# Phase one with kept weights, a later sigmoid, a copied z and B and C in a tile of their own

## The chip, the core and the metric

The kernel runs on one core of a Trainium2 chip. Its engines are TensorE (PE; the loading of its weights is PEld), VectorE (DVE), ScalarE (ACT), GpSimd (POOL) and SyncE (SP), which here issues all transfers in one queue. Each engine works through its own list of instructions in order. The metric is the device time of one execution in microseconds.

## The reference, cut to what matters

One layer of a streaming encoder on 2048 prompt frames and 32 frames of a running stream. The change lies in the first half, where the normalised input is multiplied by one input projection and the results go to two groups of heads.

```python
proj = rmsnorm(x, g_mix_pre) @ w_in            # 1024 -> q, k, v, z, xBC, dt
xbc_c = silu(causal_dwconv(xbc, ...))          # 768 channels: x 512, B 128, C 128; four taps
y = ssd_scan(x, dt, a, B, C, h0) + d_skip * x  # chunks, state carried on
y = rmsnorm(y * silu(z), g_ssm_out)
attn = stick_breaking(q, k_all, v_all)
out = concat(rmsnorm(attn, g_attn_out), y) @ w_out   # then residual, conv FFN
```

## The kernel before, in words

All products are made in pairs of halves: every operand is cut into a high part and the rest (hi, lo), and a product takes three matmuls (hi hi, lo hi, hi lo). The tokens lie along the free dimension, in four superblocks of 512, 512, 512 and 544 columns.

**Phase one** (`phase_in`, L253) runs over the superblocks. For each it

1. splits the normalised input into xhi and xlo (`split`, L315; superblock 0 in `first`, which multiplies by the norm r0 only behind the matmuls, because the norm is not there yet),
2. makes the six units of 128 channels of x, B and C, in the order 4 (B), 5 (C), 0 to 3 (x): 24 matmuls into a PSUM tile `o` of two buffers, an exit by ScalarE to `raw` (L377), a four-tap convolution on VectorE into `xc` (one `tensor_scalar`, L384, and three `scalar_tensor_tensor`, L388), a sigmoid on ScalarE (L392) and a product on VectorE (L393),
3. makes v and dt for four blocks of 128 tokens ("V", L412), two accumulators of 24 matmuls per block, each left by ScalarE (L419 or L421), in the same two buffers `o`,
4. runs the state-space scan over the blocks (`y`, `st`, `acB`, `eA`), woven into
5. the matmuls of k and q (eight units), while `prep` (L294) loads and normalises the next superblock's input,
6. makes the four units of z (`gate`, L609): a sigmoid on ScalarE and a product on VectorE both read z in PSUM (L627, L628), and a second product puts it on `xc` (L630),
7. normalises `xc` (`gate_norm`, L635) and stores it to `yS`. Only then is `xc` free for the next superblock's convolution, for it has one buffer.

The last superblock's z and norm run later, in phase two, which holds attention and the FFN.

**Weights.** `weight` (L106) fetches a unit: `raw` loads 512 KB into `wraw` (two buffers, L122), and `divide` makes the high half on ScalarE (a cast, L145) and the low half on GpSimd (a subtraction, L146), into `w` (two buffers in phase one). If a key is given, `divide` also writes both halves (1 MB) to a scratch tensor in DRAM, and a later `weight` with the same key loads them back with `recall` (L132), without ScalarE and GpSimd. In phase one no unit had a key.

**Order.** A scheduler sets the order of the instructions on each engine from the program, its dependencies and a model of durations; the order on the chip is then fixed.

Of the kernel before, what the change touches and what calls it, by code (L numbers as in the profile page):

```python
# [45 lines left out]
NSB = len(SBS)  # L46
# [23 lines left out]
class Kernel:  # L70
# [182 lines left out]
def phase_in(kn, ctx):  # L253
    nc, tc, a, o = kn.nc, kn.tc, kn.a, kn.o
# [5 lines left out]
    tmp = pool("in_tmp", 2)  # L260
    so = pool("in_out", 2)
    wp = kn.wp
# [90 lines left out]

    wfirst = kn.weight(wp, a["wbx"][4])
    for s, (t0, nt) in enumerate(SBS):
        last = s == NSB - 1
        if s == 0:
            xs, r0 = first()
            rcol = kn.rcol
# [3 lines left out]
        raw = ep.tile([P, 6, 550], F32, name="raw")  # L363
        xc = kn.xcp.tile([P, 6, 547], F32, name="xc")
        W = 547 if last else 512
        nc.vector.tensor_copy(raw[:, :, 0:3], hist[:])
        if last:
            nc.vector.tensor_copy(
                raw[:, :, 515:518], kn.cv[:, C_SST : C_SST + 18].rearrange("p (c t) -> p c t", t=3)
            )  # L370
        for c in (4, 5, 0, 1, 2, 3):
            w = wfirst if s == 0 and c == 4 else kn.weight(wp, a["wbx"][c])
            for c0, c1 in tiles_of(nt):
                ps = psd.tile([P, 512], F32, name="o")
                kn.dense(ps, w, xs, c0, c1)
                e = min(c1, 512)
                nc.scalar.copy(raw[:, c, 3 + c0 : 3 + e], ps[:, : e - c0])  # L377
                if c1 > 512:
                    nc.scalar.copy(raw[:, c, 518:550], ps[:, e - c0 : c1 - c0])
            if s == 0:  # L380
                nc.vector.tensor_tensor(raw[:, c, 3 : 3 + nt], raw[:, c, 3 : 3 + nt], r0[:, :nt], op=ALU.mult)
            y = xc[:, c, :W]
            wc = C_SW + c * 4
            nc.vector.tensor_scalar(  # L384
                y, raw[:, c, 0:W], kn.col(wc), kn.col(C_SB + c), op0=ALU.mult, op1=ALU.add
            )
            for i in range(1, 4):
                nc.vector.scalar_tensor_tensor(  # L388
                    y, raw[:, c, i : i + W], kn.col(wc + i), y, op0=ALU.mult, op1=ALU.add
                )  # L390
            t = tmp.tile([P, 550], F32, name="t")
            nc.scalar.activation(t[:, :W], y, AF.Sigmoid)  # L392
            nc.vector.tensor_tensor(y, y, t[:, :W], op=ALU.mult)  # L393
        if last:
# [11 lines left out]
        for b in range(nb):  # L406
            q = min(P, nt - b * P)
            vp = [psd.tile([P, 512], F32, name="o") for _ in range(2)]
            for h in range(2):
                for k in range(KC):  # L410
                    for i, (l, rr) in enumerate(((xhi, wv[0]), (xlo, wv[0]), (xhi, wv[1]))):
                        nc.tensor.matmul(  # L412
                            vp[h][:q, :260], l[k][:, b * P : b * P + q], rr[:, k, h * 260 : h * 260 + 260],
                            start=i == 0 and k == 0, stop=i == 2 and k == KC - 1,
                        )
            v = sd.tile([P, 520], F32, name="v")
            for dst, src in ((v[:q, 0:260], vp[0][:q, :260]), (v[:q, 260:520], vp[1][:q, :260])):
                if s == 0:
                    nc.scalar.activation(dst, src, AF.Copy, scale=rcol[:q, b : b + 1])  # L419
                else:  # L420
                    nc.scalar.copy(dst, src)  # L421
            nc.vector.tensor_tensor(
# [32 lines left out]
        ps = psm.tile([P, 512], F32, name="st")  # L455
# [17 lines left out]
        for b in range(nb):  # L473
            q = min(P, nt - b * P)
# [21 lines left out]
            for g in range(2):  # L496
                rows = slice(g * 64, g * 64 + 64)
                nc.tensor.matmul(cy[:q, g, :q], xc[rows, 4, sl], xc[rows, 5, sl], start=True, stop=True)
                for i in range(2):
                    nc.tensor.matmul(  # L500
                        cy[:, g, P + i * q : P + i * q + q],
                        h_in[rows, 2 * i : 2 * i + 2, :].rearrange("p h d -> p (h d)"), xc[rows, 5, sl],
                        start=True, stop=True,
                    )
# [26 lines left out]
            ps = psm.tile([P, 512], F32, name="st")  # L531
            nc.tensor.transpose(ps[:q, :P], xc[:, 4, sl], kn.ident[:])
            bT = sd.tile([P, P], F32, name="bT")
# [62 lines left out]
        if last:  # L596
# [3 lines left out]
            )  # L600
        bufs = {"khi": 2, "klo": 2, "t": 2, "sq": 1}
        tm = lambda nm: (so if nm in ("khi", "klo") else tmp).tile([P, 550 if nm == "t" else 544], F32, name=nm, bufs=bufs[nm])
# [6 lines left out]
def gate(kn, s, xs, xc, r0, tm):  # L609
# [3 lines left out]
    for c in range(4):  # L613
        w = kn.weight(kn.wp, kn.a["wz"][c])
        for c0, c1 in tiles:
# [7 lines left out]
            if r0 is not None:  # L623
                z = tm("t")
                nc.vector.tensor_tensor(z[:, :n], ps[:, :n], r0[:, c0:c1], op=ALU.mult)
                ps = z
            nc.scalar.activation(t[:, :n], ps[:, :n], AF.Sigmoid)  # L627
# [844 lines left out]
def build(nc, tc, a, o):  # L1472
    kn = Kernel(nc, tc, a, o)
    with ExitStack() as ctx:
# [17 lines left out]
        with ExitStack() as c2:  # L1492
            kn.wp, kn.unit, kn.wbufs, kn.rbufs = c2.enter_context(tc.tile_pool(name="weights_in", bufs=1)), KC, 2, 2
            rest = phase_in(kn, c2)
# [125 lines left out]
```

## Time and profile before

| what | us |
|---|---|
| median of three runs (lowest, highest) | 2935.15 (2931.43, 2939.62) |
| the profiled execution | 2941.02 |
| its span | 2939.2 |
| TensorE busy in the span | 2814.1 |

A row of busy time by stage has the stage, its length, then for each engine busy time and count of instructions, the granted TensorE clock, the DMA share and GB/s. A row of waits has the waiting engine, tile and line, what it waited for, and total, times and longest in us. A row of a timeline has start, duration, engine, line, operation, tiles, count, and in brackets the idle time ahead of it and what ended it. A group has busy time, mean ns of one, then idle time ahead of it and its causes. A row of the chain of waits has start, duration and what ran. Names like L161 are lines of the kernel before.

### The profile page before, as it was taken

Reading aid. Unit: us, or ns where it says so; the run is one execution under the profiler, and the core shown is the slowest. Engines: PE = TensorE matmul, PEld = TensorE weight load, DVE = VectorE, ACT = ScalarE, POOL = GpSimd, SP = SyncE. Lnnn points to the kernel's source line nnn. Section 1 sums busy time; section 2 is a strip of 40 time slices with the busy share of each in tenths; the row PEclk is TensorE's granted clock in tenths of the full one; section 3 lists DMA queues with packets and bytes.
Section 4 is the critical chain, followed back from the end, with each engine's and each line's share of the span. In section 5 each row is a group of like instructions: output and inputs, shape, how many; then the busy total and the mean of one; then the engine's idle time right before and its main releaser. Section 6 shows DMA issues by size and latency. Waiting matters only on the chain.

```text
span 2939.2 us, 46252 instructions
## 1 busy us (share of the span) xinstructions
PE 2814.1 (96%) x16771; PEld 2427.5 (83%) x16771; DVE 1690.8 (58%) x2628; ACT 1263.4 (43%) x2622; POOL 1275.4 (43%) x1131
## 2 busy tenths in 40 slices
PE   7999999989889999999999999999999999999997
PEld 6777777977788888897788888977888889999997
DVE  7667586566773555447555556675666653623333
ACT  4344444337665555446333444654444443321111
POOL 4565555435766666656322323453223233511113
PEclk9999999989999999999999999999999999999999
DMA  5646464648787778777655556656555445765556
GB/s 179 183 137 193 132 176 124 174 115 271 247 282 263 253 263 276 266 256 250 215 180 172 174 180 219 225 182 205 176 172 170 160 159 202 241 181 179 170 178 200
DMA packets 333093, 586.47 MB, mean 200 GB/s; under 512 B 73306, under 2 KB 192738, under 8 KB 332866
## 3 DMA queue, kind: packets, MB, share of 16 engines
q1 hardware_dynamic: 332866, 583.52, 62.1%
q8 instruction: 134, 2.20, 0.3%
q14 instruction: 93, 0.76, 0.1%
HBM read 445.70 MB, written 137.69 MB: 198 GB/s over the span
## 4 chain that ended last, share of the span: by engine, by line
PE 72%; DVE 13%; DMA 7%; ACT 3%; issue 2%; POOL 1%; SPq 1%; DVEq 0%; ACTq 0%; POOLq 0%
PE o L161 35%; PE u L161 12%; PE t L161 10%; PE z L863 4%; PE pa L904 4%; PE pt L882 3%; DVE xc L388 2%; DMA acB<-acD 2%; PE o L412 1%; DVE acB L488 1%; DVE prow L714 1%; DMA xr<-hS 1%; DVE xc L384 1%; DVE xlo L320 1%; DVE x L310 1%
## 5 line engine op out<-in xcount | busy, mean ns | idle before, releaser
L161 PE MATMUL o<-xhi,w 128*128 128x512 f32 (+2 forms) x3968 | 1047.9, 346 | 24.1 <-ACT xhi L334 8.0
L161 PEld LDWEIGHTS o<-xhi,w 128*128 128x128 f32 x3968 | 697.3, 191 | 119.0 <-ACT xhi L334 8.0
L161 PE MATMUL o<-xlo,w 128*128 128x512 f32 (+2 forms) x1984 | 683.8, 345 | 6.3 <-DVE xlo L320 4.2
L146 POOL TENSOR_TENSOR w<-wraw,w 128x512 fp32r<-128x512 f32 (+3 forms) x244 | 384.3, 1577 | 261.4 <-ACT w L145 232.2
L719 POOL TENSOR_TENSOR beta<-beta,prow 128x512 f32<-128x512 f32 (+3 forms) x256 | 252.5, 987 | 442.7 <-DVE prow L714 366.8
L161 PEld LDWEIGHTS o<-xlo,w 128*128 128x128 f32 x1984 | 380.0, 192 | 50.4 <-DVE xlo L320 6.1
L161 PE MATMUL u<-xhi,w 128*128 128x512 f32 x1056 | 350.3, 398 | 0.0
L161 PE MATMUL o<-ah,w 128*128 128x512 f32 x992 | 344.4, 403 | 4.3 <-DVE f L1348 3.8
L1300 POOL TENSOR_TENSOR y<-y,gb 128x512 f32<-128x512 f32 (+1 forms) x88 | 116.0, 1318 | 503.2 <-ACT gb L1299 503.1
L714 DVE TENSOR_TENSOR_SCAN prow<-gam,prow,z 128x513 f32<-128x513 f32 x192 | 245.2, 1278 | 74.1 <-ACT beta L712 69.7
L887 DVE TENSOR_TENSOR wt<-pt,wt 128x512 fp32r<-128x512 f32 (+2 forms) x320 | 191.0, 602 | 159.6 <-ACT wt L886 157.8
L886 ACT CAST wt<-pt 128x512 fp32r<-128x512 f32 (+2 forms) x320 | 166.9, 527 | 218.2 <-PE pt L882 216.3
L145 ACT CAST w<-wraw 128x512 fp32r<-128x512 f32 (+3 forms) x244 | 172.1, 705 | 170.6 <-PE o L161 98.6
L161 PEld LDWEIGHTS u<-xhi,w 128*128 128x128 f32 x1056 | 199.1, 189 | 46.8
L161 PEld LDWEIGHTS o<-ah,w 128*128 128x128 f32 x992 | 187.2, 189 | 47.0 <-DVE f L1348 6.0
L711 ACT ACTIVATE gam<-z 128x512 f32<-128x512 f32 (+2 forms) x320 | 172.3, 538 | 96.0 <-PE z L863 53.9
L161 PE MATMUL u<-xlo,w 128*128 128x512 f32 x528 | 209.5, 397 | 0.0
L161 PE MATMUL o<-al,w 128*128 128x512 f32 x496 | 196.7, 397 | 0.0
L161 PE MATMUL t<-xhi,w 128*128 128x272 f32 x960 | 189.6, 293 | 2.6 <-DMA w<-wS_up 1.7
L882 PE MATMUL pt<-ident,beta 128*128 128x128 f32 x1088 | 180.3, 277 | 4.2 <-DVE wt L887 2.7
L1292 DVE SCALAR_TENSOR_TENSOR y<-gb,cv,y 128x512 f32<-128x512 f32 (+1 forms) x176 | 142.4, 809 | 72.6 <-ACT y L1290 69.9
L904 PE MATMUL pa<-wt,v 128*64 128x256 f32 (+3 forms) x1152 | 172.3, 280 | 8.6 <-DVE wt L887 6.6
(275 smaller groups left out, 4956.4 us busy)
## 6 DMA issues: line engine op xcount, KB each, us to landing
w<-wS_up SPq DMA_DIRECT2D x264, 512.0 KB, 3.6
w<-wS_dn SPq DMA_DIRECT2D x144, 384.0 KB, 3.5
wS_up<-w SPq DMA_DIRECT2D x88, 512.0 KB, 3.4
w<-wS_out SPq DMA_DIRECT2D x78, 512.0 KB, 5.7
wraw<-wup SPq DMA_DIRECT2D x88, 256.0 KB, 4.0
k<-kS SPq DMA_DIRECT2D x80, 256.0 KB, 4.1
v<-vS SPq DMA_DIRECT2D x80, 256.0 KB, 3.8
wS_dn<-w SPq DMA_DIRECT2D x48, 384.0 KB, 3.1
```

Source lines behind the costliest of these rows:

```text
L145: nc.scalar.copy(hi, raw[:, :m, :])
L146: nc.gpsimd.tensor_tensor(lo, raw[:, :m, :], hi.bitcast(F32), op=ALU.subtract)
L161: mm = nc.tensor.matmul(ps[:, : c1 - c0], l, r, start=first and i == 0 and k == 0, stop=last and i == 2 and k == len(w) - 1, **({"skip_gro ...
L711: nc.scalar.activation(g[:, c0:512], z, AF.Sigmoid, scale=-0.125)
L714: nc.vector.tensor_tensor_scan(back(pr), back(g), z[:, 0:1].to_broadcast([P, n + 1]), self.kn.ones[:, 0:1] if prev is None else prev, op0= ...
L719: eng.tensor_tensor(b[:, :n], b[:, :n], pr[:, c0 + 1 : 513], op=ALU.mult)
L863: mm = nc.tensor.matmul(z[:, :n], q[:, P * b : P * b + P], k[:, :n], start=e == 0, stop=e == 1 and kc < s)
L882: mm = nc.tensor.transpose(t[:, P * j : P * j + P], w[:, P * j : P * j + P], kn.ident[:])
L886: nc.scalar.copy(hi, t)
L887: nc.vector.tensor_tensor(lo, t, hi.bitcast(F32), op=ALU.subtract)
L904: nc.tensor.matmul(av[:m, 2 * P * p + c0 : 2 * P * p + 2 * P], v[:, j, :m], wt[:, rest, j, c0:], start=kc == s and p + j + rest == 0, stop ...
L1292: nc.vector.scalar_tensor_tensor(y[:, :W], gb[:, i : i + W], kn.col(wc + i), y[:, :W], op0=ALU.mult, op1=ALU.add)
```

## The change

- The 24 fetches of units of x, B and C and the z units of superblocks 0 to 2 get keys. Superblock 0 writes ten units to DRAM; superblocks 1 to 3 recall x, B and C, superblocks 1 and 2 also z. Superblock 3's z has no key.
- `w` has three buffers in phase one.
- B and C go into a tile `bc` of their own; `xc` holds x alone.
- The sigmoid and product of a unit are issued after the exit of the next unit, and the last unit's after V's first block; `behind` makes each sigmoid depend on that exit, so ScalarE's list has them in this order.
- In superblocks 1 and 2 ScalarE copies z from PSUM to `zc` (two buffers), and sigmoid and product read that copy.

```diff
+    def behind(self, inst, other):
+
+        self.tc.add_manual_dep(
+            inst.ins, other.ins.name,
+            mybir.DependencyInfo(mybir.DependencyClass.NoSync, mybir.DependencyReason.DATA),
+            reason="behind",
+        )
...
-    wfirst = kn.weight(wp, a["wbx"][4])
+    wfirst = kn.weight(wp, a["wbx"][4], key=("bx", 4))
...
-        xc = kn.xcp.tile([P, 6, 547], F32, name="xc")
+        xc = kn.xcp.tile([P, 4, 547], F32, name="xc")
+        bc = kn.xcp.tile([P, 2, 547], F32, name="bc")
...
+        owed = None
+
+        def silu(y, copy):
+            t = tmp.tile([P, 550], F32, name="t")
+            kn.behind(nc.scalar.activation(t[:, :W], y, AF.Sigmoid), copy)
+            nc.vector.tensor_tensor(y, y, t[:, :W], op=ALU.mult)
+
         for c in (4, 5, 0, 1, 2, 3):
-            w = wfirst if s == 0 and c == 4 else kn.weight(wp, a["wbx"][c])
+            w = wfirst if s == 0 and c == 4 else kn.weight(wp, a["wbx"][c], key=("bx", c))
...
-                nc.scalar.copy(raw[:, c, 3 + c0 : 3 + e], ps[:, : e - c0])
+                copy = nc.scalar.copy(raw[:, c, 3 + c0 : 3 + e], ps[:, : e - c0])
...
-            y = xc[:, c, :W]
+            y = xc[:, c, :W] if c < 4 else bc[:, c - 4, :W]
...
-            t = tmp.tile([P, 550], F32, name="t")
-            nc.scalar.activation(t[:, :W], y, AF.Sigmoid)
-            nc.vector.tensor_tensor(y, y, t[:, :W], op=ALU.mult)
+            if owed is not None:
+                silu(owed, copy)
+            owed = y
...
+            if b == 0:
+                silu(owed, copy)
...
-        bufs = {"khi": 2, "klo": 2, "t": 2, "sq": 1}
+        bufs = {"khi": 2, "klo": 2, "t": 2, "sq": 1, "zc": 2}
...
-        w = kn.weight(kn.wp, kn.a["wz"][c])
+        w = kn.weight(kn.wp, kn.a["wz"][c], key=("z", c) if s < NSB - 1 else None)
...
+            elif s < NSB - 1:
+                z = tm("zc")
+                nc.scalar.copy(z[:, :n], ps[:, :n])
+                ps = z
...
-            kn.wp, kn.unit, kn.wbufs, kn.rbufs = c2.enter_context(tc.tile_pool(name="weights_in", bufs=1)), KC, 2, 2
+            kn.wp, kn.unit, kn.wbufs, kn.rbufs = c2.enter_context(tc.tile_pool(name="weights_in", bufs=1)), KC, 3, 2
```

The matmuls that read B and C (L498, L500, L532) read `bc` in place of `xc`. The scheduler orders the whole program anew. In the changed kernel's list the lines have moved on: L393 is the exit to `raw` (L377 before), L153 a unit's cast (L145), L384 the sigmoid (L392), L385 its product (L393), L437 the exit of v (L421), L169 the dense matmuls (L161), L428 those of V (L412), L516 and L518 the first matmuls of the scan (L498, L500).

ScalarE in superblock 0, kernel before, from the exit of unit C on (`wvhi` is a quarter of V's weights, `r_229` the norm r0):

```order
L377 COPY raw<-o 128x512
L145 CAST w<-wraw 128x1024
L303 ACTIVATE sq<-x 128x512
L377 COPY raw<-o 128x512
L145 CAST w<-wraw 128x1024
L248 COPY r_229<-st 128x512
L283 CAST wvhi<-wvraw 128x1040
L377 COPY raw<-o 128x512
L145 CAST w<-wraw 128x1024
L283 CAST wvhi<-wvraw 128x1040
L377 COPY raw<-o 128x512
L145 CAST w<-wraw 128x1024
```

The same stretch in the changed kernel, from the copy of r0 on:

```order
L256 COPY r_231<-st 128x512
L393 COPY raw<-o 128x512
L153 CAST w<-wraw 128x1024
L384 ACT_TABLE_LOAD
L384 ACTIVATE t<-bc 128x512
L153 CAST w<-wraw 128x1024
L384 ACTIVATE t<-bc 128x512
L291 CAST wvhi<-wvraw 128x1040
L384 ACTIVATE t<-xc 128x512
L153 CAST w<-wraw 128x1024
L393 COPY raw<-o 128x512
```

The exit in the second row is that of the fourth unit; the casts behind it are those of the fifth and sixth units and of the first unit of k. Before, the fifth unit's cast stood ahead of the copy of r0 and of the fourth unit's exit, and no sigmoid among them.

TensorE in superblock 0, kernel before, at the first matmul of the scan, which stands behind V's first block:

```order
L412 MATMUL o<-wvhi,xhi_168 128x260
L412 MATMUL o<-wvhi,xlo_176 128x260
L412 MATMUL o<-wvlo,xhi_168 128x260
L498 MATMUL y<-xc 128x128
L412 MATMUL o<-wvhi,xhi_161 128x260
```

In the changed kernel, at the same matmul:

```order
L169 MATMUL o<-xhi_170,w 128x512
L169 MATMUL o<-xhi_163,w 128x512
L169 MATMUL o<-xlo_171,w 128x512
L516 MATMUL y<-bc 128x128
L518 MATMUL y<-bc,hT_150 128x128 x2
L169 MATMUL o<-xhi_163,w 128x512
```

It now stands after the second matmul of the sixth unit, ahead of all of V.

ScalarE in superblock 1, kernel before, in V:

```order
L421 COPY v<-o 128x260 x2
L392 ACT_TABLE_LOAD
L392 ACTIVATE t<-xc 128x512 x2
L421 COPY v<-o 128x260 x2
L392 ACTIVATE t<-xc 128x512 x2
L421 COPY v<-o 128x260
L392 ACTIVATE t<-xc 128x512 x2
```

In the changed kernel:

```order
L393 COPY raw<-o 128x512
L153 CAST w<-wraw 128x1024
L384 ACTIVATE t<-xc 128x512
L437 COPY v<-o 128x260
L384 ACTIVATE t<-xc 128x512 x2
L437 COPY v<-o 128x260
L384 ACTIVATE t<-xc 128x512
L314 ACTIVATE t<-x 128x512
L437 COPY v<-o 128x260
```

B's and C's sigmoids stand ahead of this stretch now, and x's four are spread over V's first three exits.

More of the change, by code (lines that the diff above doesn't have):

```diff
@@ L376, in phase_in @@
                 e = min(c1, 512)
-                nc.scalar.copy(raw[:, c, 3 + c0 : 3 + e], ps[:, : e - c0])
+                copy = nc.scalar.copy(raw[:, c, 3 + c0 : 3 + e], ps[:, : e - c0])
                 if c1 > 512:
-                    nc.scalar.copy(raw[:, c, 518:550], ps[:, e - c0 : c1 - c0])
+                    copy = nc.scalar.copy(raw[:, c, 518:550], ps[:, e - c0 : c1 - c0])
             if s == 0:
                 nc.vector.tensor_tensor(raw[:, c, 3 : 3 + nt], raw[:, c, 3 : 3 + nt], r0[:, :nt], op=ALU.mult)
-            y = xc[:, c, :W]
+            y = xc[:, c, :W] if c < 4 else bc[:, c - 4, :W]
             wc = C_SW + c * 4
@@ L418, in phase_in @@
                 if s == 0:
-                    nc.scalar.activation(dst, src, AF.Copy, scale=rcol[:q, b : b + 1])
+                    copy = nc.scalar.activation(dst, src, AF.Copy, scale=rcol[:q, b : b + 1])
                 else:
-                    nc.scalar.copy(dst, src)
+                    copy = nc.scalar.copy(dst, src)
+            if b == 0:
+                silu(owed, copy)
             nc.vector.tensor_tensor(
@@ L497, in phase_in @@
                 rows = slice(g * 64, g * 64 + 64)
-                nc.tensor.matmul(cy[:q, g, :q], xc[rows, 4, sl], xc[rows, 5, sl], start=True, stop=True)
+                nc.tensor.matmul(cy[:q, g, :q], bc[rows, 0, sl], bc[rows, 1, sl], start=True, stop=True)
                 for i in range(2):
@@ L501, in phase_in @@
                         cy[:, g, P + i * q : P + i * q + q],
-                        h_in[rows, 2 * i : 2 * i + 2, :].rearrange("p h d -> p (h d)"), xc[rows, 5, sl],
+                        h_in[rows, 2 * i : 2 * i + 2, :].rearrange("p h d -> p (h d)"), bc[rows, 1, sl],
                         start=True, stop=True,
@@ L531, in phase_in @@
             ps = psm.tile([P, 512], F32, name="st")
-            nc.tensor.transpose(ps[:q, :P], xc[:, 4, sl], kn.ident[:])
+            nc.tensor.transpose(ps[:q, :P], bc[:, 0, sl], kn.ident[:])
             bT = sd.tile([P, P], F32, name="bT")
```

## The prediction

> **What bounds the kernel now.** I read the profile page first, then the busy time by stage, TensorE's waits in the first 680 us, the chain of waits, and single engines' timelines where a wait begins.
>
> ```profile
> span 2939.2 us, 46252 instructions
> PE 2814.1 (96%) x16771; PEld 2427.5 (83%) x16771; DVE 1690.8 (58%) x2628; ACT 1263.4 (43%) x2622; POOL 1275.4 (43%) x1131
> PE 72%; DVE 13%; DMA 7%; ACT 3%; issue 2%; POOL 1%; SPq 1%; DVEq 0%; ACTq 0%; POOLq 0%
> ```
>
> TensorE bounds the whole; a change of phase one (0 to 645 us) can only win the time in which TensorE stands or runs slow there. The stages of superblock 0 (x, B, C; then V), of superblock 1 (x, B, C; then V) and the end of the phase:
>
> ```profile
> core 0: us, PE busy (x) PEld busy (x) DVE busy (x) ACT busy (x) POOL busy (x), PEclk, DMA share, GB/s
> 8.00:49.00 41.00, 39.07 (x162) 31.08 (x163) 32.24 (x32) 23.41 (x33) 19.16 (x8) 1.00 0.60 214
> 49.00:81.00 32.00, 27.05 (x200) 25.61 (x199) 22.14 (x30) 12.26 (x23) 16.65 (x14) 0.95 0.40 100
> 180.00:213.00 33.00, 33.00 (x151) 26.30 (x150) 15.87 (x16) 16.30 (x23) 22.01 (x13) 1.00 0.67 224
> 213.00:241.00 28.00, 25.06 (x196) 23.68 (x195) 22.64 (x33) 12.28 (x23) 18.85 (x12) 1.00 0.42 107
> 566.00:645.00 79.00, 71.41 (x545) 65.11 (x544) 48.34 (x120) 25.76 (x48) 28.92 (x18) 0.89 0.55 161
> ```
>
> TensorE is full while it makes x, B and C, and loses 3 to 5 us in each V stage (third number of a row against the second). Its waits (total, times, longest):
>
> ```profile
> PE o L412 <- ACT v L421: 8.9, 3, 3.4
> PE o L161 <- ACT xhi L334: 8.0, 1, 8.0
> PE o L161 <- DVE t L628: 5.1, 2, 2.6
> PE o L161 <- DVE xlo L320: 4.2, 3, 1.8
> PE o L412 <- ACT v L419: 3.2, 2, 2.3
> PE o L412 <- ACT raw L377: 1.7, 1, 1.7
> PE o L161 <- ACT raw L377: 1.4, 1, 1.4
> PE o L412 <- ACT raw L379: 0.9, 1, 0.9
> ```
>
> The 8.0 us are the start and stay. The waits for v and raw come from ScalarE's order, here in superblock 1:
>
> ```profile
> 216.38 0.38 ACT L421 COPY v<-o 128x260 f32<-128x260 f32 x1 [2.47 <-PE o L412]
> 223.34 1.29 ACT L392 ACTIVATE t<-xc 128x512 f32<-128x512 f32 x2 [5.28 <-DVE xc L388]
> 224.54 0.63 ACT L421 COPY v<-o 128x260 f32<-128x260 f32 x2
> ```
>
> ScalarE stands 5.28 us in a sigmoid that waits for VectorE's convolution; two finished V accumulators lie behind it and both buffers of o are full. VectorE is late because xc is free only after the gated norm of the superblock before:
>
> ```profile
> L384 DVE TENSOR_SCALAR xc<-raw,cv 128x512 f32<-128x512 f32 (+1 forms) x24 | 24.8, 1075 | 18.4 <-POOL klo L656 18.4
> L145 ACT CAST w<-wraw x68: 1027/1051/1070, 6.0 to 632.6; 128x1024 fp32r<-128x1024 f32 x68
> L146 POOL TENSOR_TENSOR w<-wraw,w x68: 2357/2407/6562, 7.1 to 633.8; 128x1024 fp32r<-128x1024 f32 x68
> 38.10 0.54 DVE L384 TENSOR_SCALAR xc<-raw,cv 128x512 f32<-128x512 f32 x1
> 39.39 2.65 POOL L146 TENSOR_TENSOR w<-wraw,w 128x1024 fp32r<-128x1024 f32 x1 [2.97 <-ACT w L145]
> 39.70 3.08 DVE L384 TENSOR_SCALAR xc<-raw,cv 128x512 f32<-128x512 f32 x2
> ```
>
> It idles 18.4 us for that over three superblocks. The last three rows show a second brake: a VectorE instruction of 0.54 us, begun while a weight's subtraction (2.4 us) runs on GpSimd, ends only with it (two of them take 3.08 us where 1.1 would do).
>
> **The change, part by part.** Sums are against the profiled run (2941.0 us; 1.8 us outside its span), which lies 5.9 us above the median of the three runs, 2935.15; I take the same difference off that median.
>
> *V exits, superblocks 1 to 3.* B and C are convolved into their own tile without waiting for the norm, 26 subtractions (18 for x, B, C, 8 for z; 63 us of GpSimd at 2.4) go, and each sigmoid stands behind the next exit. B's and C's ten instructions (for each one of 0.5 us, three and a product of 0.7, some 7 us for both) move into VectorE's idle time, and the norm should end some 3 us sooner, because the subtractions that stand between its own on GpSimd are gone. So x's four groups (13 us) should be through about ten us sooner than now. V's exits fall due every 3 us (24 matmuls, half of the 5.92 us of 48 below; the row at 216.38 is the second one in superblock 1); by the new order one sigmoid stands ahead of the first, two ahead of the second, one ahead of the third, and all four are ready by then. Removed: 8.9 + 0.9 us at V and 1.4 at raw; I leave 1 for late ones: **-10.2** (bounds -11.2 and -3).
>
> *z exits, superblocks 1 and 2.* TensorE waits for VectorE's product from PSUM (5.1). ScalarE now empties the bank with eight more copies, beside eight casts of 1.05 us that go:
>
> ```profile
> L352 ACT COPY kf<-o 128x512 f32<-128x512 f32 (+1 forms) x32 | 15.4, 482 | 44.2 <-PE o L161 33.4 <-POOL rn_v L226 6.5 <-POOL klo L585 3.8
> L628 DVE TENSOR_TENSOR t<-o,t x8: 674/678/692, 317.8 to 491.8; 128x512 f32<-128x512 f32 x8
> ```
>
> The copy (0.5 us) frees the bank with VectorE eight x products behind; two zc buffers let TensorE run two units ahead. **-5** (bounds -5.1 and 0).
>
> *xlo at the borders.* TensorE gets there sooner, VectorE too, without z's subtractions. From 4.2: **-1** (bounds -2.5 and +3).
>
> *Clock.* After such a wait TensorE runs slow for a while:
>
> ```profile
> 67.06 7.45 PE o L412 x48
> 74.92 5.92 PE o L412 x48
> 81.70 5.81 PE o L161 x24
> 318.59 7.41 PE o L161 x24
> ```
>
> 48 matmuls of V take 1.5 us more after a wait of 2.3 us (the granted clock of that stage is 0.95, not 1.00), and 24 of z take 1.6 more after 2.6. Not every wait shows it (superblock 1's V stage has 1.00); I count it at two or three of the waits that go in superblocks 1 to 3: **-4** (bounds -6 and 0). [...]
>
> *Superblock 0* pays. Its unit loads, exits and the two engines stand so:
>
> ```profile
> SPq L122 <- POOL w L146: 163.5, 46, 9.9
> 34.45 3.73 DVE L381 TENSOR_TENSOR raw<-raw,r 128x512 f32<-128x512 f32 x3 [5.89 <-ACT r L248]
> 37.78 0.59 ACT L377 COPY raw<-o 128x512 f32<-128x512 f32 x1 [2.40 <-PE o L161]
> 42.71 2.07 DVE L388 SCALAR_TENSOR_TENSOR xc<-raw,cv,xc 128x512 f32<-128x512 f32 x3
> 43.30 1.06 ACT L283 CAST wvhi<-wvraw 128x1040 fp32r<-128x1040 f32 x1 [3.98 <-DMA wvraw<-wv]
> 48.79 0.29 PE L412 MATMUL o<-wvhi,xhi 128*128 128x260 f32 x1
> ```
>
> Ten writes of 1 MB wait in SyncE's queue for a subtraction; the raw loads behind them waited for the same one already (163.5 us), but their data now come behind 1 MB more. (a) The fifth unit's cast now follows the fourth's exit: 38.4 + 1.05 + 2.4 = 41.8 until its low half stands, 4 us after TensorE ended the fourth; two matmuls with the high half fit in: +3.5. (b) The sixth unit's cast follows B's sigmoid. VectorE starts at about 34, when r is there, and by the new order B's convolution ends after 14 instructions (three scalings of raw, three of 0.54 us, eight of 0.7) and one blockade of 2 us: about 44. Sigmoid (0.65), cast and subtraction give 48, and the first y<-bc, now after two matmuls of the sixth unit, waits for C's product, about 49. TensorE comes there at 41.8 + 24 x 0.24 = 47.6: +1.4, 2 with some slow matmuls behind it. (c) The last quarter of V's weights, cast at 43.30 until now, loads behind the sixth write, so after 48; V needs its low half 20 matmuls (2.4 us) after it starts: +2. Off go V's own waits, 3.2 + 1.7, and 1.5 of clock: net **+1** (bounds -5 and +9).
>
> *Recalls.* 18 for x, B, C and 8 for z, 1 MB each; no row shows one. The nearest:
>
> ```profile
> DMA to landing us min/median/max: 2.6/3.7/8.8
> w<-wS_out SPq DMA_DIRECT2D x78, 512.0 KB, 5.7
> ```
>
> Those are 0.5 MB: bounds 2.6 and 17.6 (twice the longest); I take 2 x 3.7 = 7.4. With three buffers a recall is issued when TensorE leaves the unit three before, two units or 11.6 us ahead: **0**. What queues behind a waiting recall (x of the next superblock, yS stores) has the same cover.
>
> *Superblock 3's tail* (79 us with 71 busy, state chain against k and q) and phase two keep their order but for a few rows: **0** (bounds -3 and +3).
>
> Sum: -10.2 - 5 - 1 - 4 + 1 = -19.2: 2941.0 becomes 2921.8, and the median **2916**.
>
> **Rivals.** 0.3% (8.8 us) is what a measurement here can tell from no change.
> 1. *Superblock 0 loses more*: ScalarE's queue holds two weight casts behind sigmoids, and VectorE is slower than I reckon. At the bound of +9 the sum is -11.2: 2924. For it: rows 34.45 and 39.70; against: the same V waits vanish later.
> 2. *The wait moves to xlo.* VectorE is full where a superblock ends; the z product now reads two SBUF operands. If each of the eight lasts as long as a GpSimd instruction beside it (the 39.70 row), VectorE is 1.5 to 2 us later per product and TensorE waits for xlo what it saved at z (+5), without the -1 (+1), and 3 more at the bound: sum -10.2, 2925. [...]
> 3. *Slower: recalls come late.* Place: each superblock's first units, where 2 MB of x share the queue. Price: landing minus 11.6, at the bound 6 us for three units in three superblocks, 54: 2970. It decides from a landing of 11.6 us; 19 us are lost when those nine are 2.1 late. Against: DMA share 0.67 in 180 to 213.
> 4. *The exits stay blocked*: sigmoids still stand between V's copies, and if the norm frees xc no sooner the waits stay: -10.2 becomes -3 and the clock term -1.5: 2926.
>
> **How the numbers follow.** Forecast 0.58; rival 1 0.14; rival 2 0.10; rival 3 0.09; rival 4 0.06; two of 1, 2 and 4 together, about 2935, 0.03. Low end: every bound of gain, -11.2 - 5.1 - 2.5 - 6 - 5 = -29.8, and 1 in the tail: 2904. High end 2935, where two rivals meet; beyond lies rival 3. The cases near 2925 lie on the bound of 2926.3 and are split: faster 0.55 of the forecast, 0.09 of rival 1, 0.06 of rival 2, 0.03 of rival 4, together 0.73; slower rival 3 and 0.01 that nothing here names, 0.10; same the rest, 0.17.
>
> **What would show it.** Right: no wait for v in superblocks 1 to 3, none of TensorE for t at z, convolution of bc before 200 us, phase one ending near 626; new waits of 2 to 5 us on w and on bc near 38 to 50 us. Wrong: waits on DMA w<-wS (rival 3), xlo waits above 8 us (2), TensorE reaching V later than 58 us (1), sigmoids with idle time ahead of V's copies (4).

## The result, and the profile after

The changed kernel takes 2918.76 us (median of four runs, 2917.37 to 2923.97), the kernel before beside it 2935.71 (four runs, 2931.43 to 2939.62): a ratio of 0.9947, 95% interval 0.9931 to 0.9963. The profiled execution took 2923.97 us. The page of the changed kernel, in the same rows as before:

```profile
span 2922.2 us, 46225 instructions
PE 2808.3 (96%) x16771; PEld 2428.2 (83%) x16771; DVE 1667.7 (57%) x2628; ACT 1246.6 (43%) x2604; POOL 1203.1 (41%) x1105
PE 77%; DVE 10%; DMA 7%; issue 2%; ACT 2%; SPq 1%; POOL 1%; DVEq 0%; POOLq 0%; ACTq 0%
```

GpSimd has 72 us less to do and VectorE 23, with as many instructions on VectorE as before. That is the first hint of what the change does. The first matmul z of phase two is at 646.28 before (first row, kernel before) and at 626.30 after (second row, changed kernel): phase one is 20.0 us shorter and the span 17.0, so phase two gives back 3.

```profile
646.28 0.22 PE L863 MATMUL z<-k,qa 128*128 128x128 f32 x1
```

```profile
626.30 0.22 PE L885 MATMUL z<-k,qa 128*128 128x128 f32 x1
```

In both kernels TensorE does the same 3509 matmuls up to there. The rows of that whole stretch, before and after:

```profile
0.00:646.28 646.28, 592.18 (x3509) 495.12 (x3510) 427.73 (x710) 268.74 (x427) 330.87 (x207) 0.97 0.54 158
```

```profile
0.00:626.30 626.30, 583.17 (x3509) 492.30 (x3510) 404.31 (x709) 250.63 (x409) 261.77 (x181) 0.98 0.64 202
```

So 11.0 of the 20.0 us are idle time of TensorE (54.1 us before, 43.1 after), and 9.0 are the same matmuls run faster, at a granted clock of 0.98 in place of 0.97.

The stages after, with the columns shown of before (x, B, C and V of superblock 0; x, B, C and V of superblock 1; the end of the phase):

```profile
8.00:56.00 48.00, 41.48 (x164) 32.03 (x165) 41.19 (x44) 25.39 (x37) 18.24 (x8) 0.93 0.84 310
56.00:83.00 27.00, 24.96 (x201) 24.16 (x200) 14.60 (x19) 11.51 (x20) 18.04 (x13) 1.00 0.49 137
180.00:209.00 29.00, 29.00 (x125) 23.01 (x123) 17.53 (x19) 12.94 (x18) 13.31 (x9) 1.00 0.71 261
209.00:236.00 27.00, 26.18 (x206) 24.93 (x204) 16.25 (x22) 10.74 (x21) 18.31 (x14) 1.00 0.39 109
547.00:629.00 82.00, 71.64 (x577) 65.71 (x573) 50.77 (x124) 29.01 (x54) 28.58 (x17) 0.94 0.57 161
```

By the first matmul of each stage, superblock 0's first stage is 8 us longer and its V 6 us shorter; V of superblock 1 now has TensorE busy for 26.18 of 27. TensorE's waits up to 680 us:

```profile
PE y L518 <- DVE hT L580: 9.3, 4, 2.6
PE st L550 <- DVE hT L580: 6.1, 3, 3.1
PE o L169 <- POOL w L154: 3.8, 2, 2.4
PE o L428 <- ACT v L437: 3.3, 2, 2.4
PE o L428 <- ACT raw L393: 3.2, 1, 3.2
PE y L556 <- DVE acB L528: 2.7, 2, 2.3
PE o L169 <- ACT w L153: 1.6, 1, 1.6
```

The wait for t at z (5.1) and the border waits for xlo (4.2) are gone; V's exits in superblocks 1 to 3 went from 9.8 to 6.5 us (with raw's at the units of x, from 11.2 to 6.7); and TensorE now runs into the scan's state hT for 15.4 us, where the kernel before had 8.7:

```profile
PE st L532 <- DVE hT L562: 4.6, 2, 3.5
PE y L500 <- DVE hT L562: 4.1, 6, 1.6
```

What superblock 0 pays is seen on ScalarE: the fifth unit's cast behind the fourth exit, then a sigmoid that waits 4.39 us for B's convolution, and the sixth unit's cast behind that.

```profile
37.97 1.05 ACT L153 CAST w<-wraw 128x1024 fp32r<-128x1024 f32 x1
43.40 1.28 ACT L384 ACT_TABLE_LOAD   x1 [4.39 <-DVE bc L404]
44.70 0.63 ACT L384 ACTIVATE t<-bc 128x512 f32<-128x512 f32 x1
45.23 1.03 ACT L153 CAST w<-wraw 128x1024 fp32r<-128x1024 f32 x1
```

So far most of this looks like the forecast. The experiments give another account of it.

### The profile page after: what moved, and what is told of

The parts are those of the page before. It is cut to its first block, busy times and chain, and to the rows that moved or that the text cites. A ratio compares the mean times of both kernels' runs of the same rounds, so it can differ in the third digit from the quotient of the medians.

```text
span 2922.2 us, 46225 instructions
## 1 busy us (share of the span) xinstructions
PE 2808.3 (96%) x16771; PEld 2428.2 (83%) x16771; DVE 1667.7 (57%) x2628; ACT 1246.6 (43%) x2604; POOL 1203.1 (41%) x1105
## 4 chain that ended last, share of the span: by engine, by line
PE 77%; DVE 10%; DMA 7%; issue 2%; ACT 2%; SPq 1%; POOL 1%; DVEq 0%; POOLq 0%; ACTq 0%
PE o L169 38%; PE u L169 12%; PE t L169 10%; PE z L885 4%; PE pa L926 4%; PE pt L904 3%; PE o L428 3%; DVE acB L506 1%; DVE xc L404 1%; DMA xr<-hS 1%; DVE prow L736 1%; DVE xc L560 1%; DMA w<-wS_up 1%; DMA acB<-acD 1%; DVE xlo L1074 1%
## 5 line engine op out<-in xcount | busy, mean ns | idle before, releaser
L169 PE MATMUL o<-xhi,w 128*128 128x512 f32 (+2 forms) x3968 | 1050.4, 346 | 21.8 <-ACT xhi L342 7.8
L169 PEld LDWEIGHTS o<-xhi,w 128*128 128x128 f32 x3968 | 700.8, 192 | 115.0 <-ACT xhi L342 7.8
L169 PE MATMUL o<-xlo,w 128*128 128x512 f32 (+2 forms) x1984 | 684.7, 345 | 2.1 <-DVE xlo L343 1.1
L169 PEld LDWEIGHTS o<-xlo,w 128*128 128x128 f32 x1984 | 380.7, 192 | 45.1 <-DVE xlo L343 1.6
L154 POOL TENSOR_TENSOR w<-wraw,w 128x512 fp32r<-128x512 f32 (+3 forms) x218 | 313.9, 1443 | 206.9 <-ACT w L153 186.0
L169 PE MATMUL u<-xhi,w 128*128 128x512 f32 x1056 | 350.1, 397 | 0.0
L169 PE MATMUL o<-ah,w 128*128 128x512 f32 x992 | 344.1, 403 | 4.6 <-DVE f L1370 3.8
L169 PEld LDWEIGHTS u<-xhi,w 128*128 128x128 f32 x1056 | 199.2, 189 | 46.9
L169 PEld LDWEIGHTS o<-ah,w 128*128 128x128 f32 x992 | 187.0, 189 | 47.1 <-DVE f L1370 5.7
L153 ACT CAST w<-wraw 128x512 fp32r<-128x512 f32 (+3 forms) x218 | 145.1, 666 | 166.9 <-PE o L169 111.5
L169 PE MATMUL u<-xlo,w 128*128 128x512 f32 x528 | 209.5, 397 | 0.0
L169 PE MATMUL o<-al,w 128*128 128x512 f32 x496 | 196.6, 396 | 0.0
L169 PE MATMUL t<-xhi,w 128*128 128x272 f32 x960 | 187.4, 291 | 2.6 <-DMA w<-wS_up 1.7
```

Source lines behind the costliest of these rows:

```text
L153: nc.scalar.copy(hi, raw[:, :m, :])
L154: nc.gpsimd.tensor_tensor(lo, raw[:, :m, :], hi.bitcast(F32), op=ALU.subtract)
L169: mm = nc.tensor.matmul(ps[:, : c1 - c0], l, r, start=first and i == 0 and k == 0, stop=last and i == 2 and k == len(w) - 1, **({"skip_gro ...
```

## The experiments

I call the three parts W (weights kept, three buffers), S (each sigmoid behind the next exit, B and C apart) and Z (z copied). All times are medians, and each ratio is to the kernel before on the same chip. "To 853" and "853 to 1825" compare the profiled runs with the kernel before: the third and the ninth group of phase two in which TensorE spreads a norm factor (matmuls u out of rn_v and the identity), at 852.8 and 1825.3 us in the kernel before. "Rows moved" is how many of VectorE's instructions of phase two stand elsewhere in its list than in the kernel before; no kernel changes phase two's code. "Phase one" is TensorE's busy and idle time up to its 3509th matmul in the profiled run, in us (592.2 + 54.1 in the kernel before). It is one execution each: changed and after_order2, or no_w and no_w_order1, whose phase one differs only by eight copies and the order that they cause, lie up to 3.5 us apart in either part.

| kernel | parts | us | ratio (95% interval) | phase one: busy + idle | to 853 | 853 to 1825 | rows moved |
|---|---|---|---|---|---|---|---|
| changed | W S Z | 2918.8 | 0.9947 (0.9931 to 0.9963) | 583.2 + 43.1 | -18.8 | +3.7 | 18 |
| w_alone | W | 2922.8 | 0.9940 (0.9922 to 0.9958) | 589.2 + 47.1 | -10.3 | -0.1 | 7 |
| s_alone | S | 2952.4 | 1.0038 (1.0024 to 1.0052) | 596.9 + 55.9 | +7.9 | +6.5 | 394 |
| z_alone | Z | 2929.0 | 0.9967 (0.9952 to 0.9982) | 583.6 + 52.7 | -16.3 | +0.6 | 13 |
| no_w | S Z | 2965.3 | 1.0080 (1.0060 to 1.0100) | 592.8 + 59.2 | +7.9 | +17.3 | 493 |
| w_z | W Z | 2926.3 | 0.9950 (0.9935 to 0.9964) | 585.6 + 48.3 | -15.8 | +2.9 | 195 |
| w_s | W S | 2937.9 | 0.9990 (0.9977 to 1.0003) | 588.5 + 39.5 | -20.3 | +16.1 | 493 |
| pool_again | W S Z, GpSimd's work back | 2931.9 | 0.9966 (0.9953 to 0.9979) | 592.8 + 51.3 | -12.2 | +6.4 | 22 |
| act_again | W S Z, ScalarE's work back | 2910.0 | 0.9896 (0.9879 to 0.9912) | 591.7 + 41.9 | -20.8 | 0.0 | 15 |
| after_order2 | W S Z, other order | 2933.7 | 0.9989 (0.9977 to 1.0001) | 586.7 + 41.5 | -18.3 | +15.9 | 506 |
| no_w_order1 | S Z, order back | 2947.4 | 1.0029 (1.0016 to 1.0041) | 590.2 + 62.4 | +8.5 | +0.1 | 13 |
| keys2 | W S Z, two buffers | 2915.7 | 0.9919 (0.9900 to 0.9938) | 577.3 + 42.4 | -24.8 | -1.4 | 1 |
| all_kept | W S Z, k and q kept too | 2902.5 | 0.9883 (0.9865 to 0.9902) | 573.2 + 26.4 | -44.1 | +3.9 | 18 |

### Each part alone, and W undone

W alone, against the kernel before (the z units' keys and the first fetch's likewise):

```diff
-            w = wfirst if s == 0 and c == 4 else kn.weight(wp, a["wbx"][c])
+            w = wfirst if s == 0 and c == 4 else kn.weight(wp, a["wbx"][c], key=("bx", c))
-            kn.wp, kn.unit, kn.wbufs, kn.rbufs = c2.enter_context(tc.tile_pool(name="weights_in", bufs=1)), KC, 2, 2
+            kn.wp, kn.unit, kn.wbufs, kn.rbufs = c2.enter_context(tc.tile_pool(name="weights_in", bufs=1)), KC, 3, 2
```

> Of the four edits only the weights are made: x, B, C and z kept in DRAM, three weight buffers; sigmoids right behind their convolution, B and C in one tile with x, z read from PSUM as before. Theory A (the forecast's steps): no wait of TensorE in superblocks 1 to 3 named a cast or a subtraction of weights, so the recalls give nothing there beyond 1 to 3 us of clock and border, and superblock 0 pays: the fifth and sixth casts late, as in the changed kernel (xBC of superblock 0 near 48 us, not 41, V of it near 27, not 33); total 2934 to 2937 beside 2935.7 before, V's and z's waits as before (8 to 11 and 5 us). Rival B: the 26 casts and 26 subtractions taken out are what frees ScalarE and GpSimd, and most of the gain of 17 us is theirs: 2922 to 2926, V's waits half gone.

2922.76 us, 0.994: my theory A falls, rival B holds in its time. (The ranges were set beside 2935.7 us; the kernel before took 2940.67 beside these runs, so the gain of 18 us is rather more than B had.) But not by its reason: the waits for V's exits in superblocks 1 to 3 are all still there (9.3 and 0.8 us, where the kernel before had 8.9 and 0.9; TensorE's waits of w_alone up to 680 us), while those for t at z and for xlo at the borders are gone without any copy of z.

```profile
PE y L516 <- DVE hT L578: 9.7, 5, 3.3
PE o L428 <- ACT v L437: 9.3, 7, 2.7
PE o L428 <- ACT raw L395: 0.8, 1, 0.8
```

S alone, against the kernel before (`silu` and the second tile as in the change):

```diff
-            t = tmp.tile([P, 550], F32, name="t")
-            nc.scalar.activation(t[:, :W], y, AF.Sigmoid)
-            nc.vector.tensor_tensor(y, y, t[:, :W], op=ALU.mult)
+            if owed is not None:
+                silu(owed, copy)
+            owed = y
```

> Only the sigmoids' edit: each behind the next unit's exit, B and C in a tile of their own; weights loaded and divided in each superblock with two buffers, z read from PSUM. Theory A: V's waits in superblocks 1 to 3 go from 11 us to 5 to 6, superblock 0 keeps its order, the border and z waits stay: 2926 to 2931. Rival B (the weights free ScalarE): V's exits stay behind casts, 2932 to 2936.

2952.42 us, 1.0038: slower. Both theories had it between nothing and a gain. Where it loses is seen at the border from superblock 0 to 1. First the changed kernel, then s_alone: the norm's last subtraction on GpSimd, and VectorE's first instruction on x, which waits for it, and in s_alone also the wait of V that follows.

```profile
202.86 2.35 POOL L678 TENSOR_TENSOR klo<-xc,khi 128x512 fp32r<-128x512 f32 x2
205.25 3.55 DVE L400 TENSOR_SCALAR xc<-raw,cv 128x512 f32<-128x512 f32 x3 [5.67 <-POOL klo L678]
```

```profile
213.25 1.29 POOL L674 TENSOR_TENSOR klo<-xc,khi 128x512 fp32r<-128x512 f32 x1 [3.39 <-PE o L169]
214.50 4.93 POOL L154 TENSOR_TENSOR w<-wraw,w 128x1024 fp32r<-128x1024 f32 x2
214.58 2.60 DVE L400 TENSOR_SCALAR xc<-raw,cv 128x512 f32<-128x512 f32 x1 [8.75 <-POOL klo L674]
226.99 0.59 PE L428 MATMUL o<-wvhi,xhi 128*128 128x260 f32 x1 [5.19 <-ACT v L437]
```

x's tile comes free 9.3 us later than in the changed kernel and 7.1 later than in the kernel before (207.49), and its first instruction then takes 2.60 us beside two weight subtractions. Of the 7.1 us, 3.4 are GpSimd's wait for TensorE ahead of the norm's last subtraction (the first row of s_alone). V's exit, behind x's sigmoid, is 5.19 us late. And VectorE's work before it was slow as well (groups of one shape up to 660 us, mean ns behind the comma; changed kernel, then s_alone):

```profile
L404 DVE SCALAR_TENSOR_TENSOR bc<-raw,cv,bc 128x512 f32<-128x512 f32 x18 | 14.0, 789 | 0.3
L328 DVE TENSOR_TENSOR xlo<-x,xhi 128x512 fp32r<-128x512 f32 x16 | 10.2, 684 | 0.0
```

```profile
L404 DVE SCALAR_TENSOR_TENSOR bc<-raw,cv,bc 128x512 f32<-128x512 f32 x18 | 25.0, 1400 | 0.3
L328 DVE TENSOR_TENSOR xlo<-x,xhi 128x512 fp32r<-128x512 f32 x16 | 19.2, 1248 | 0.0
```

The same instructions take 1.8 times as long where GpSimd still subtracts weights. S moves B's and C's convolutions into that stretch, and the four products of the norm behind them end at 205.5, where they ended at 201.9 in the kernel before. So S alone saves TensorE no idle time in phase one (55.9 us, 54.1 before), and beside Z it costs some (59.2, z_alone 52.7). Part of its loss lies in phase two, whose order it moved as well.

Z alone is the four lines of the change in `gate` and nothing else:

```diff
+            elif s < NSB - 1:
+                z = tm("zc")
+                nc.scalar.copy(z[:, :n], ps[:, :n])
+                ps = z
```

> Only the copy of z by ScalarE in superblocks 1 and 2. Theory A: the 5.1 us that TensorE waits at z for VectorE's product out of PSUM goes, nothing else moves: 2929 to 2932. Rival: the copy only moves the wait to a later unit on the same two buffers, 2934 to 2936.

2929.03 us, 0.9967: in theory A's range, and the rival falls. But beside 2940.67 the gain is 12 us, twice what A had, and A's mechanism doesn't carry it: the wait for t is gone, yet TensorE's idle time in phase one fell by 1.4 us only, and the same matmuls took 8.6 us less. Why they ran faster stays open.

W undone in the changed kernel:

```diff
-            w = wfirst if s == 0 and c == 4 else kn.weight(wp, a["wbx"][c], key=("bx", c))
+            w = wfirst if s == 0 and c == 4 else kn.weight(wp, a["wbx"][c])
-            kn.wp, kn.unit, kn.wbufs, kn.rbufs = c2.enter_context(tc.tile_pool(name="weights_in", bufs=1)), KC, 3, 2
+            kn.wp, kn.unit, kn.wbufs, kn.rbufs = c2.enter_context(tc.tile_pool(name="weights_in", bufs=1)), KC, 2, 2
```

> The changed kernel with the weights' part undone: no weights kept, two weight buffers; sigmoids behind the next exit, B and C apart, z copied by ScalarE. Theory A: the weights' part is worth about nothing or less (superblock 0 pays 7 us at xBC and gets it back in V): 2917 to 2921 beside 2918.8 of the changed kernel. Rival B: the weights' part carries the gain: 2927 to 2933. Should the parts only work together (each opens a wait that the other closes), this one and the three parts alone each give less than 4 us and their sum falls short of 17 by far.

2965.25 us, 1.008, more than any theory had. The parts do not add: S alone +12, Z alone -12, both +25 in medians. Two things were still mixed up here, what GpSimd does to VectorE and what happens in phase two (853 to 1825: +17.3).

### Two parts at a time

S undone, then Z undone, in the changed kernel (the diffs above, backwards).

> The changed kernel with the sigmoids' part undone (each sigmoid right behind its convolution, B and C in x's tile); weights kept, z copied. After the first four runs the theory is P: the gain is GpSimd's. The 26 subtractions of weights that the recalls leave out stood at the borders of superblocks beside VectorE's norm, xlo and convolutions and slowed them, and held back the last subtraction of the norm, which frees x's tile. By P the sigmoids' edit is worth 0 to 4 us once the weights are kept: 2914 to 2922. By theory A (the forecast's) V's exits stay blocked in superblocks 1 to 3, 8 to 10 us: 2924 to 2930.

> The changed kernel with z read from PSUM again in superblocks 1 and 2; weights kept, sigmoids behind the next exit. If z's copy is worth what it gave alone (9 to 10 us) and the parts add: 2926 to 2930. If it is worth only the wait for t (5 us): 2922 to 2925. If the weights' part already frees VectorE there: 2917 to 2920, and no wait for t at z is seen.

w_z takes 2926.34 us, in A's range, and A's mechanism is there: TensorE still waits 9.7 us at V's exits in superblocks 1 to 3 (6.5 in the changed kernel). Beside W, S does shorten phase one: TensorE's idle time goes from 48.3 to 43.1 us with Z and from 47.1 to 39.5 without. But little of it is left behind phase one (to 853 the changed kernel leads w_z by 3.0 us), and against the kernel before beside it the ratio of w_z is 0.9950, the changed kernel's 0.9947: S, beside W and Z, hardly changes the whole time. w_s takes 2937.88 us, slower than all three expectations. Yet up to 853 us w_s is as early as the changed kernel (-20.3 against -18.8), and no wait for t at z is in its trace: with W, the copy of z is worth nothing in phase one. It loses 16 us behind 853, in code that it shares with the changed kernel word for word. no_w and w_s, with 493 rows moved, lose 16 to 17 us there and s_alone, with 394, 6.5; w_z, with 195, loses 2.9; kernels with 22 or fewer lie between -1.4 and +6.4.

### Is it GpSimd's work or ScalarE's?

Both kernels are the changed one with extra work, in `recall`; the second has `nc.scalar.copy(idle[:], hi)` in the last line.

```diff
+        if keys[0][0] in ("bx", "z"):
+            hi, lo = w[:, 0, :m, :].bitcast(F32), w[:, 1, :m, :].bitcast(F32)
+            idle = pool.tile([P, m, P], F32, name="idle")
+            self.nc.gpsimd.tensor_tensor(idle[:], hi, lo, op=ALU.subtract)
```

> The changed kernel, and for each of the 26 recalled units GpSimd subtracts its two halves into a tile that nobody reads, as large as the subtraction that the recall saved; extra work only. Theory P: VectorE is slowed again at the borders (xlo's mean from 0.70 back to 0.8 to 1.1 us, the convolutions of B and C from 0.82 towards 1.5) and the time goes back to 2932 to 2950. Rival C (the casts taken from ScalarE, or the third buffer, carry the gain): 2917 to 2923.

> The changed kernel, and for each of the 26 recalled units ScalarE copies its high half into a tile that nobody reads, as long as the cast that the recall saved; extra work only. Theory P: 2917 to 2924, ScalarE has room. Rival C: 2928 to 2940, V's exits wait behind the copies again.

GpSimd's work back: 2931.88 us, just under P's range (0.9966; the changed kernel's interval ends at 0.9963, its own begins at 0.9953, so the two ratios alone would not part them; act_again's does). By the ratios a third of the changed kernel's gain is lost (0.34% faster than the kernel before, not 0.53%). ScalarE's work back: 2910.01 us, not slower at all. The two kernels up to the same matmul as above, pool_again first:

```profile
0.00:644.11 644.11, 592.81 (x3509) 497.21 (x3510) 444.02 (x710) 250.07 (x409) 340.28 (x214) 0.97 0.62 196
```

```profile
0.00:633.57 633.57, 591.68 (x3510) 498.38 (x3511) 403.67 (x710) 273.76 (x435) 260.93 (x188) 0.96 0.64 200
```

TensorE's idle time is 51.3 us with GpSimd's work back and 41.9 with ScalarE's; it was 43.1 in the changed kernel and 54.1 before. Behind phase one pool_again makes up 11 us on the changed kernel in the stretch to 853, over the same 1359 matmuls: busy 179.0 us at a granted clock of 0.96, against 187.6 at 0.92. That is why so much less is lost in the whole time than in phase one. In 82 to 565 us, pool_again and its groups:

```profile
82.00:565.00 483.00, 455.10 (x2569) 376.41 (x2568) 334.97 (x515) 182.57 (x299) 270.51 (x155) 0.96 0.61 191
```

```profile
L408 DVE SCALAR_TENSOR_TENSOR bc<-raw,cv,bc 128x512 f32<-128x512 f32 x18 | 19.3, 1083 | 0.4
L332 DVE TENSOR_TENSOR xlo<-x,xhi 128x512 fp32r<-128x512 f32 x16 | 17.1, 1115 | 0.0
```

The same stretch of the kernel before, and of the changed one:

```profile
82.00:565.00 483.00, 451.37 (x2585) 370.20 (x2584) 323.00 (x518) 202.08 (x318) 263.20 (x159) 0.98 0.53 156
```

```profile
82.00:565.00 483.00, 464.70 (x2730) 389.09 (x2730) 303.62 (x539) 192.86 (x316) 202.17 (x140) 0.99 0.64 202
```

In 483 us the changed kernel does 145 matmuls and 21 VectorE instructions more, with VectorE 19 us less busy, for GpSimd is 61 us less busy; with GpSimd's work back VectorE is at 335 and TensorE at 2569 matmuls. That is theory P: 8.2 of the 11.0 us of idle time come back with GpSimd's work and none with ScalarE's, so rival C falls. Slow VectorE instructions are one part of it. Another is GpSimd itself: in pool_again its extra subtractions stand ahead of the norm's (three of them, 7.98 us, from 194.88), and x's tile comes free at 211.22, not 205.25; the run doesn't part the two. ScalarE's copies have no such cost in idle time, but the matmuls of phase one took 8.5 us longer in that execution, the slowest of act_again's six. Why act_again beats the changed kernel by 0.5% I did not find. Its phase-one lists differ from the changed kernel's by more than the copies, as the scheduler wrote them, so a single difference of some 10 us between two of these kernels proves little by itself.

### Is it the order of phase two?

The same edit in the changed kernel and in no_w; it puts eight idle copies on ScalarE in superblock 3:

```diff
+    spare = c1p.tile([P, 512], F32, name="spare")
+    nc.gpsimd.memset(spare[:], 0.0)
...
                 nc.scalar.copy(hi[:, :nt], kf[:, :nt])
+                for _ in range(4 if last and c == 3 else 0):
+                    nc.scalar.copy(spare[:, :512], kf[:, :512])
```

> The changed kernel with eight copies of a k or q unit by ScalarE (0.6 us each, read by nobody) in superblock 3. Their use is that the scheduler then writes VectorE's list of phase two another way: 506 of its rows stand elsewhere than before the change, as in the two kernels that lost 18 us in phase two (weights undone, z undone), where the changed kernel has 18. Theory O: the order of phase two costs these 18 us: 2932 to 2940, phase one as in the changed kernel. Rival: those kernels lost by what they undid, the order is harmless: 2918 to 2924.

> The kernel with the weights' part undone (sigmoids later, B and C apart, z copied; nothing kept, two weight buffers), with the same eight copies by ScalarE, which here bring VectorE's list of phase two back to the order of the kernel before (13 rows elsewhere, 493 without them). Theory O: 2942 to 2950, some 18 us under the 2965 of the same kernel without the copies, phase one about 6 us later than the kernel before. Rival: 2962 to 2970.

Both as theory O had it. The changed kernel goes to 2933.67 us with the other order, 0.9989 instead of 0.9947, the intervals apart; up to 853 it is the same (-18.3), and then it loses 15.9. The kernel without W comes back from 2965.25 to 2947.37, all of it behind 853 (+0.1 instead of +17.3). TensorE's waits from 834 to about 1400 us, in the changed kernel (834 to 1399) and in after_order2 (834 to 1421):

```profile
PE z L885 <- DVE prow L736: 4.1, 5, 1.5
PE o L169 <- DVE f L1370: 1.7, 2, 1.0
```

```profile
PE z L889 <- DVE rn_v L228: 5.6, 1, 5.6
PE o L169 <- DVE f L1374: 4.7, 3, 3.5
PE o L169 <- ACT xhi L1077: 2.6, 1, 2.6
PE pa L930 <- DVE wt L913: 2.2, 2, 2.0
```

In the second order TensorE waits longer for VectorE, for a norm (rn_v 5.6) and for the residual f. From 853 to 1825 it is idle for 25.2 us, 14.8 in the changed kernel, and busy for 963.2 and 961.5: most of the loss is waiting, in code that is the same. With the order equal, W is worth 1.0029 - 0.9947 = 0.82% beside S and Z, some 24 us, and Z about nothing beside W and S (w_s 0.9990, after_order2 0.9989, both in the second order).

### The third buffer

```diff
-            kn.wp, kn.unit, kn.wbufs, kn.rbufs = c2.enter_context(tc.tile_pool(name="weights_in", bufs=1)), KC, 3, 2
+            kn.wp, kn.unit, kn.wbufs, kn.rbufs = c2.enter_context(tc.tile_pool(name="weights_in", bufs=1)), KC, 2, 2
```

> The changed kernel with two weight buffers again; keys, recalls and all else as changed. VectorE's order of phase two is the changed kernel's but for 17 rows. In the changed kernel's trace the recalls of x, B and C take 4.8 us from issue to landing and those of z 5.1 (medians). With two buffers a recall can be issued only when the unit two back has left TensorE, some 5.6 us (24 matmuls of 0.233) before its own turn. Theory R: that leaves 0.5 to 0.8 us and the slower half of 26 recalls come late by 1 to 2 us each, plus slow matmuls behind: 2928 to 2940, with waits of TensorE for w's landing in superblocks 1 to 3. Rival: the landing fits, the third buffer is worth nothing: 2916 to 2922.

2915.74 us; the interval (0.9900 to 0.9938) overlaps the changed kernel's. The time is just under the rival's range, and theory R holds in its mechanism alone: recalls do come late seven times, 4.8 us in all. TensorE's idle time in phase one is 42.4 us all the same, for its waits for the state are 7.6 us, where the changed kernel has 15.4; so the run shows that two buffers do as well here, and not what the third is worth by itself. Issue to landing (median us, last column) in the changed kernel, then the wait in keys2:

```profile
w<-wS_bx SPq DMA_DIRECT2D x18, 1024.0 KB, 4.8
w<-wS_z SPq DMA_DIRECT2D x8, 1024.0 KB, 5.1
```

```profile
PE o L169 <- DMA w<-wS_bx: 4.8, 7, 1.3
```

### Keeping k and q as well

If P is right, GpSimd's subtractions for k and q beside the scan cost too. The same eight idle copies keep the first order.

```diff
-                w = kn.weight(wp, a[name][c])
+                w = kn.weight(wp, a[name][c], key=(name, c))
```

> The changed kernel with k's and q's eight units kept in DRAM as well (24 recalls more, as many casts and subtractions less), and the same eight copies, with which VectorE's list of phase two has the changed kernel's order but for 11 rows. Theory P: GpSimd's 24 subtractions of 2.4 us beside the scan slow VectorE there (acB, eA, the state), and TensorE's 15 us of waits for the state shrink by half: 2905 to 2914. Rival: the scan's waits are its own chain and the 24 MB more of reads come late beside it: 2918 to 2935.

2902.53 us, 0.9883 (0.9865 to 0.9902): the fastest of all, 16 us under the changed kernel and better than P asked for. Its waits for the state up to 680 us, and VectorE's largest group of the scan, in the changed kernel and here:

```profile
PE st L552 <- DVE hT L582: 1.8, 2, 1.4
```

```profile
L506 DVE TENSOR_SCALAR acB<-acB,acum 128x128 f32<-128x128 f32 x128 | 44.5, 412 | 29.4 <-DMA acB<-acD 29.4
```

```profile
L508 DVE TENSOR_SCALAR acB<-acB,acum 128x128 f32<-128x128 f32 x128 | 33.9, 335 | 23.9 <-DMA acB<-acD 23.9
```

15.4 us of waits became 1.8, and TensorE's idle time in phase one went from 43.1 to 26.4. The scan's chain was not at its own limit. At V's exits of superblocks 1 to 3 TensorE waits 0.6 us here, for raw. The recalls take k's and q's casts from ScalarE as well; no run parts the two for these units, so that GpSimd's share carries this gain is argued from pool_again and act_again, not shown.

## Why the prediction was right, and where it wasn't

The time was right (2916 forecast, 2918.8 measured, in the range, faster by more than 0.3%), and the waits it named fell by 13.8 us (V's exits and raw 4.5, z 5.1, xlo 4.2) of the 16.2 that it booked for them. The account behind it was wrong: what it booked on S comes only with W, and without W S costs time. That the sum still came out within 3 us is luck: too little at V, and losses that it didn't have (the scan, phase two), were made up by more at xlo and by matmuls that ran faster than it reckoned.

- **V exits (-10.2).** In the changed kernel -4.5 (11.2 to 6.7 us). The step that failed is "all four are ready by then". The norm did free x's tile sooner (205.25, before 207.49), and in superblock 1 x's groups were through at 223.5 in place of 233.4, about the ten us that were forecast. But VectorE began several of x's units before it ended one, and the first of x's sigmoids, which now stands ahead of V's exits, came only 9 to 10 us after x's tile was free. Here in superblock 2, where V's first matmul is at 358.2 and TensorE then waits 2.44 us for an exit:

```profile
355.11 3.53 DVE L400 TENSOR_SCALAR xc<-raw,cv 128x512 f32<-128x512 f32 x3 [4.99 <-POOL klo L678]
```

```profile
365.44 1.35 ACT L384 ACTIVATE t<-xc 128x512 f32<-128x512 f32 x2 [5.50 <-DVE xc L404]
```

  The term's other premise, that "B's and C's ten instructions move into VectorE's idle time", holds only with W: S alone costs 12 us (some 8 of them before 853), because the ten instructions then run beside the subtractions (the multiply-adds of 128x512 take 1.40 us on average there, 0.79 in the changed kernel). The forecast named the subtractions, as help for this term; that their going is worth more, in VectorE's work and GpSimd's own at the borders, it did not see.
- **z exits (-5).** The wait went. But W alone removes that wait too, and beside W and S the copy is worth about nothing: the step took for the copy's what W removes anyway.
- **xlo (-1).** Mis-sized: all 4.2 us went, for xlo takes 0.68 us in place of 1.29 (kernel before, below).
- **Clock (-4).** Mis-sized as far as can be told: the matmuls of phase one are busy for 9.0 us less, at a granted clock of 0.98 in place of 0.97, and from 646 to 853 for 4.6 us more. No run had the clock apart, and z_alone's matmuls ran faster by as much (8.6 us), so what made them faster stays open.
- **Superblock 0 (+1).** The first stage +8.0, V -6.3, together +1.7. (a) came: TensorE waits 1.6 us for the fifth unit's cast and 2.4 for its low half, where 3.5 was reckoned. Behind that wait the unit's matmuls ran slow (0.43 us each at first, 0.23 later), which (a) left out. (b) did not come as a wait: the sixth cast is at 45.23 and the low half stands at 49.0, but TensorE, late from the fifth unit, comes to the sixth only at 49.9. (c) was 0.6, not 2. V starts between 55.5 and 56.8 us in every kernel with W, keys2 among them: it is the keys, not the third buffer.
- **Recalls (0).** Right: landings of 4.8 and 5.1 us, where I took 7.4, and no wait for one in phase one. Rival 3 was far off, and even two buffers cost nothing that was measured.
- **Superblock 3's tail and phase two (0).** The changed kernel gave 3 us back in phase two, at the bound of 3. What I did not see is the risk: "keep their order but for a few rows" holds for this kernel by luck. A neighbour with one part less, or eight idle copies more, has 500 rows moved and loses 16 us.
- **Not in the sum:** the scan's waits for its state, +6.7 us.

VectorE's xlo in the kernel before, for the shape shown of the others:

```profile
L320 DVE TENSOR_TENSOR xlo<-x,xhi 128x512 fp32r<-128x512 f32 x16 | 19.8, 1285 | 0.0
```

Rivals 1 and 4 each have a piece in the changed kernel (the 8 us of superblock 0; the sign named for rival 4, sigmoids with idle time ahead of V's copies, with 6.5 us left at V). Rival 2 has none: no wait for the border's xlo is left. None came about as a time.

## What to carry to other kernels

When one engine's busy time falls without fewer instructions, ask which other engine got quieter: here GpSimd's subtractions cost time in VectorE's work (xlo 1.12 us with them put back, 0.68 without) and in GpSimd's own list (x's tile free at 211.22, not 205.25) that TensorE's waits did not name. Take the parts of a change apart before crediting one of them, two at a time as well, for here one part gains only behind another. Set TensorE's idle time apart from the time in which it is busy: over the same matmuls the busy time moved by 9 us and more between kernels, and in phase one it was the idle time that told GpSimd's work from ScalarE's (51.3 us with the one put back, 41.9 with the other). And where a scheduler writes the order, compare the order of the code that was not touched: 500 moved rows in phase two cost 16 us, as much as the whole change gained.

## What the runs showed of the hardware

Four groups of VectorE's instructions took longer in kernels in which GpSimd had more to subtract, two of them by far more than I reckoned. The multiply-add of B's and C's convolution took 0.79 us on average with 26 weight subtractions gone, 1.08 with as much work put back and 1.40 in s_alone; xlo 0.68, 1.12 and 1.25. With ScalarE's work put back instead (act_again) the two took 0.79 and 0.69. The other two are tensor_scalars: the one that opens B's and C's convolution took 0.55, 0.65 and 0.97 us in the same three kernels, acB's 0.41 in the changed kernel and 0.34 with k and q kept. Not every group did: the multiply-add of x's convolution took 1.05, 1.03 and 0.94 us in those three. (All are means up to 660 us, for the shapes 128x512 and, of acB, 128x128.) The prediction's row at 39.70, from which rival 2 has its price, is a tensor_scalar as well, not z's product. That product took 0.68 to 0.69 us reading z's copy in the changed kernel (eight of them), and as long out of PSUM before; but GpSimd ran nothing beside six of the eight, so what its work does to this product was not shown.
